# Loading and splitting all four blocks of the last gate weight inside the last expert's loop instead of one

## The chip, the cores and the metric

The kernel runs on one core of a Trainium2 chip. The metric is the device time of one execution in microseconds, the median of several executions. One further execution is profiled: its trace holds the start and the end of every instruction on every engine, every transfer, and the clock that TensorE was granted. Names of engines: PE is TensorE (PEld its weight loads), DVE is VectorE, ACT is ScalarE, POOL is GpSimd, and SP is the queue that issues the transfers.

## What is computed

The reference is a trunk of two layers for 256 tokens of width 1024 in f32. Each layer is an attention mixer, a layer norm, a channel mixer, a layer norm and a per-layer gate. Only the end of the second layer matters here: its channel mixer is a top-2-of-8 mixture of experts, and its gate is what the kernel computes last.

```
for e in range(N_EXPERTS):                                   # moe_swiglu, layer 1
    out = out + gates[..., e:e+1] * ((silu(x @ w_gate[e]) * (x @ w_up[e])) @ w_down[e])
x = layer_norm(alpha * x + out, ln_ffn_g, ln_ffn_b)
x = x + (p[i] @ w_ple_proj[i]) * sigmoid(x @ w_ple_gate[i])  # w_ple_gate[i]: 1024 x 1024
```

Each expert has three matrices of 1024 x 3584 f32, so the eight experts are the bulk of what the program reads.

## The kernel before

**Blocks and their order.** All expert weights come in blocks of 1 MB (128 partitions x 2048 f32). `main_experts` writes the order of the blocks out by hand in the list `seq`. An expert's hidden width is cut into four chunks (`CHUNKS`: 4, 8, 8 and 8 pieces of 128). A chunk of 8 pieces has eight blocks `("w", e, f, h)`, each with half a block of the gate and half of the up weight (two transfers of 512 KB, line 994), and then four blocks `("d", e, f, h)` of the down weight (one transfer each, line 121). The down blocks of a chunk stand in the list behind the w blocks of the next chunk. The step `("p", 7, 1, 0)` stands behind the down blocks of the last expert's chunk 0, and thus ahead of the w blocks of chunk 2. It carries the first of the four blocks of `w_ple_gate`, each 1 MB, which `ple_gate_blocks` lists.

**Loads.** `take(n)` issues the loads of the list, in its order, as far ahead as the ring of raw buffers has slots; `load` shrinks that ring near the end, to 18 and then to 8 slots, because the buffers are needed for other things. All loads go through one queue, SP, in program order. A load waits until the PE (or the split) has read what was in its slot.

**PE work.** Step `w` makes matmuls on L895 (`gate_up_quads`), step `d` makes matmuls on L882 and L885 (`down_quads`). `in_order` pins the order of the instructions on PE, DVE, ACT and POOL to the program's order in this loop. At the end of a chunk ACT and DVE compute silu, product and transpose (L1030 to L1035).

**Splits.** The final gate works in pairs of f32r parts: `hi` is a rounded copy made on ACT (L139), `lo` is the difference made on DVE (L143). In step `p` the first gate block is split in pieces of 1024 columns.

**The ending.** `ending` runs behind the loop. It issues the load of the second gate block, the two layer-norm parameter rows (`ln_params`, L292), and the third and fourth gate block, finishes the last down block, scatters the expert's result into `y` (L862 on PE, L865 on DVE), normalises token tile 0 (L300 to L311), transposes it (L279), and multiplies it with the gate weight (`gate_step`, L1457; token tile 1 in `gate_mm`, L1447 to L1450). Calls `high(k)` and `low(k)` put the twelve splits of the three late blocks, in pieces of 512 columns, between these operations on ACT and DVE.

Of the kernel before, what the change touches and what calls it, by code (L numbers as in the profile page):

```python
# [34 lines left out]
NE = 8  # L35
# [5 lines left out]
CB = 512  # L41
# [22 lines left out]
def trunk(ctx: ExitStack, tc: tile.TileContext, a: dict, out: bass.AP):  # L64
# [7 lines left out]
    def acc_bank(name):  # L72
        return ps.tile([P, CB], F32, tag="acc", bufs=4, name=name)

    def gu_bank(name):
        return ps.tile([P, CB], F32, tag="gu", bufs=2, name=name)
# [11 lines left out]
    rings, used = {}, {}  # L88
# [38 lines left out]
    def w_parts(loaded, piece):  # L127

        raw, nk, cols, name = loaded
        pool, tag, size = ring_slot("hl")  # L130
        hi = pool.tile([P, 2048], F32R, tag=tag + "hi", bufs=size, name=f"hi_{name}")
        lo = pool.tile([P, 2048], F32R, tag=tag + "lo", bufs=size, name=f"lo_{name}")
        n = nk * cols

        pieces = [slice(i * piece, (i + 1) * piece) for i in range(n // piece)]

        def high(i):
            cs = pieces[i]
            nc.scalar.activation(hi[:, cs], raw[:, cs], AF.Copy)  # L139

        def low(i):
            cs = pieces[i]
            nc.vector.tensor_tensor(lo[:, cs], raw[:, cs], hi[:, cs].bitcast(F32), op=ALU.subtract)  # L143

        return (hi[:, :n].rearrange("p (k c) -> p k c", c=cols),
                lo[:, :n].rearrange("p (k c) -> p k c", c=cols)), high, low

    def w_split(loaded, piece=1024):
        unit, high, low = w_parts(loaded, piece)
        for i in range(loaded[1] * loaded[2] // piece):  # L150
            high(i)
            low(i)
        return unit
# [13 lines left out]
    @contextmanager  # L167
    def in_order(engines=("PE", "DVE", "Activation", "Pool")):

        traced = nc.cur_bb.bb.instructions  # L170
        start = len(traced)
        yield
        for e in engines:
            last = None
            for ins in traced[start:]:
                if ins.engine == getattr(mybir.EngineType, e):
                    if last is not None:
                        tc.add_manual_dep(ins, last.name, mybir.DependencyInfo(
                            mybir.DependencyClass.NoSync, mybir.DependencyReason.DATA), reason="in_order")
                    last = ins  # L180
# [591 lines left out]
    def moe(i, x, xT, router, pj):  # L772
        j = i // 2
        with tc.tile_pool(name=f"route{i}", bufs=1, reuse_waits="tile") as rp:
            xT = [transposed(x[t], t, f"b{i}", rp, ("y", "zraw")[t]) for t in range(NT)]
            y = []
            hls = standing[1] + second[1]
            spare = hls[3:]
# [143 lines left out]
            def main_experts(p1, name, first):  # L922
# [2 lines left out]
                small = [r >= SMALL for r in RANKS]  # L925
                pe, peT, ob, hT = slots(0, p1, False), None, None, {}
                groups = [(CS if v else CM) // CG for v in small]
                which, loaded, hooks = {}, [], {}

                def gathered(e, h, bank):  # L930

# [20 lines left out]
                h = first(xe, pe)  # L952
# [8 lines left out]
                seq, ahead = [], None  # L961
                for e in range(NE):
                    for f, (_, nb) in enumerate(CHUNKS):
                        if ahead:

                            seq += [("w", e, f, h) for h in range(nb)]
                            seq += [("d", *ahead, h) for h in range(CHUNKS[ahead[1]][1] // 2)]
                        if (e, f) == (NE - 1, 1):
                            seq.append(("p", e, f, 0))
                        ahead = e, f  # L970
                seq += [("d", *ahead, h) for h in range(CHUNKS[ahead[1]][1] // 2)]

                def block_of(m, e, f, h):
                    if m == "p":
                        return ple_gate_blocks(i)[h]
                    if e and e not in which:
                        which[e] = nc.values_load(ordi[0:1, e:e + 1], engines=[mybir.EngineType.SP],
                                                  min_val=0, max_val=NE - 1)
                    off = which.get(e, e) * (D * DFF) + j * NE * D * DFF
                    b0, nb = CHUNKS[f]  # L980
                    if m == "d":
                        return (dram(a["w_exp_down"], off, [[1, 1]]), (b0 + 2 * h) * P, 2, D, 0, D,
                                f"d{name}{e}{f}{h}", 2 if (e, f, h) == seq[-1][1:] else 1)
                    nk = 8 // nb
                    return [dram(a[w], off + h * nk * P * DFF + b0 * P, [[DFF, P], [P * DFF, nk], [1, nb * P]])
                            for w in ("w_exp_gate", "w_exp_up")], nk, f"w{name}{e}{f}{h}"
# [10 lines left out]
                def load():  # L997

                    block, n = seq[len(loaded)], len(loaded)
                    gone = ()  # L1000
                    if n == 26:
                        gone = ("y",)
                    if n == len(seq) - 26:
                        gone = ("z", "ln", "xT0", "xT1", "w0hi", "w0lo", "w1hi", "w1lo", "w2hi", "w2lo")
                    if block[0] == "p":
                        gone = (spare[0][1] + "hi", spare[0][1] + "lo")
                    rings["raw"] = [z for z in rings["raw"] if z[1] not in gone]
                    loaded.append((gate_up_load if block[0] == "w" else w_load)(*block_of(*block)))
# [13 lines left out]
                def run(n, when):  # L1022
                    for fn in hooks.pop((n, when), []):
                        fn()
# [83 lines left out]
                with in_order():  # L1108
                    for n in range(len(seq)):
                        run(n, "pre")  # L1110
                        m, e, f, h = seq[n]
                        half = take(n)
                        run(n, "mid")
                        if n == len(seq) - 1:
                            break
                        if (m, e, f, h) == ("w", 0, 1, 3):
                            p1, gates[:] = order(gates)
                        if m == "w":
                            if h == 0:
                                banks = [acc_bank(f"w{name}{e}{f}{v}") for v in range(groups[e])]  # L1120
                            nk = half.shape[1]
                            for k in range(nk * h, nk * h + nk):
                                gate_up_quads(banks, xe, k, half[:, k % nk], k == 0, k == KD - 1)
                            if k == KD - 1:
                                token_step(e, f, banks)
                                slots_next(n, e, f)
                                if f == len(CHUNKS) - 1 and e + 1 < NE:
                                    next_expert(n, e + 1)
                        if m == "d":
                            if f == 0 and h == 0:  # L1130
                                ob = [gu_bank(f"eo{name}{e}{c}") for c in range(1 if small[e] else 2)]
                            for k in range(2 * h, 2 * h + 2):
                                edge = f == k == 0, (f, k) == (len(CHUNKS) - 1, CHUNKS[-1][1] - 1)
                                if small[e]:

                                    for r in range(2):
                                        for q in range(4):
                                            c, g = divmod(q, 2)
                                            nc.tensor.matmul(ob[0][q * CG:(q + 1) * CG, r * CQ:(r + 1) * CQ],  # L1139
                                                             hT[e, f][:, g, k, :],  # L1140
                                                             half[:, k % 2, c * CB + r * CQ:c * CB + (r + 1) * CQ],
                                                             start=edge[0] and r == 0, stop=edge[1] and r == 1)
                                else:
                                    down_quads(ob, hT[e, f], k, half, *edge)
                            if edge[1]:
                                scatter(n, e, ob, peT)
                        if m == "p":
                            rings["hl"] = [spare[0]]
                            use_slots("hl")
                            early = [w_split(loaded[n])]  # L1150
                        run(n, "post")
                    assert not hooks
                    ending(hT[seq[-1][1:3]], ob, peT, early, half)
# [267 lines left out]

            lns = []
            main_experts(pos1, "e", first_chunk)

            over = nc.values_load(left[0:1, 0:1], min_val=-C, max_val=S)
# [59 lines left out]
    loaded = [w_load(*kv[0], parts=2)]  # L1485
# [62 lines left out]
```

## Time and profile before

| | |
|---|---|
| time, median of 3 runs | 1348.99 us (1348.56 to 1349.21) |
| time of the profiled execution | 1348.58 us |
| span of the profiled execution (first to last instruction) | 1346.9 us, so 1.7 us lie around it |
| PE busy | 1311.2 us, 97% of the span |
| DVE, ACT busy | 431.6 us (32%), 318.9 us (24%) |
| SP's transfers | 434.72 MB, 82.6% of what 16 engines could carry in the span |
| mean granted clock of TensorE | 0.993 |

Times in the rows below are microseconds from the start of the span. A clock of 1.00 is 2.4 GHz, 0.50 is 1.2 GHz. The loop over the experts ends near 1299, the gate's first matmul starts at 1310.71, and the last operation on the output ends near 1337.6.

### The profile page before, as it was taken

How to read it: one execution, taken by the hardware profiler on the slowest of the kernel's cores; microseconds unless marked ns; L12 is line 12 of the kernel's file. 1: busy time of each engine (PE TensorE's matmuls, PEld its weight loads, DVE VectorE, ACT ScalarE, POOL GpSimd, SP SyncE). 2: the span in 40 equal slices, each digit the busy share in tenths (PEclk: the TensorE clock that was granted, in tenths of full speed). 3: DMA queues.
4: the chain of work that ended last, by engine and by line, in shares of the span. 5: the costliest groups of instructions: out<-in, count | busy, mean ns of one | idle time of the engine just before them, and what ended most of it. 6: DMA issues, size and time to landing. Idle time of an engine off the chain costs nothing.

```text
span 1346.9 us, 29881 instructions
## 1 busy us (share of the span) xinstructions
PE 1311.2 (97%) x12815; PEld 764.5 (57%) x12815; DVE 431.6 (32%) x843; ACT 318.9 (24%) x609; POOL 12.9 (1%) x38
## 2 busy tenths in 40 slices
PE   8999999999999999999999999999999998899986
PEld 6778888888787744453543443463543453343445
DVE  7777444445767711011010010102011011011045
ACT  6865444434458300010000000001000000001012
POOL 1000000000000000000000000000000000000000
PEclk9999999999999999999999999999999999999988
DMA  9438555535358799999999999999999999999961
GB/s 326 164 114 309 191 187 188 187 125 188 126 190 287 264 379 368 394 378 418 415 418 419 415 417 419 414 414 414 411 416 418 410 413 417 412 414 414 417 266 37
DMA packets 141364, 436.79 MB, mean 324 GB/s; under 512 B 11808, under 2 KB 12576, under 8 KB 141216
## 3 DMA queue, kind: packets, MB, share of 16 engines
q1 hardware_dynamic: 141216, 434.72, 82.6%
q8 instruction: 105, 1.72, 0.5%
q14 instruction: 43, 0.35, 0.1%
HBM read 433.63 MB, written 1.05 MB: 323 GB/s over the span
## 4 chain that ended last, share of the span: by engine, by line
PE 65%; DMA 32%; DVE 2%; issue 0%; ACT 0%; SPq 0%; DVEq 0%; ACTq 0%
DMA raw_we<-in_w_exp_up_dram 24%; PE we L895 19%; PE eoe L882 7%; DMA raw_de<-in_w_exp_down_dram 7%; PE gf L159 2%; PE gf L160 2%; PE gf L161 2%; PE uf L160 2%; PE uf L161 2%; PE uf L159 2%; PE eoe L1139 2%; PE fo L159 2%; PE fo L160 2%; PE fo L161 2%; PE qkv L161 2%; PE qkv L160 2%
## 5 line engine op out<-in xcount | busy, mean ns | idle before, releaser
L895 PE MATMUL we<-raw_we,xs_e 128*32 128x512 f32 (+1 forms) x5184 | 508.8, 545 | 7.0 <-DMA raw_we<-in_w_exp_up_dram 7.0
L895 PEld LDWEIGHTS we<-raw_we,xs_e 128*32 128x32 f32 x5184 | 166.4, 110 | 319.5 <-issue 281.8
L1033 DVE TENSOR_TENSOR sgh<-we,sgh 128x256 f32<-128x256 f32 (+1 forms) x81 | 32.0, 395 | 590.3 <-ACT sgh L1030 588.7
L882 PE MATMUL eoe<-raw_de,hT 128*32 128x256 f32 x2520 | 186.5, 379 | 0.0
L885 PE MATMUL eoe<-raw_de,hT 128*32 128x256 f32 x840 | 185.3, 379 | 0.0
L1030 ACT ACTIVATE sgh<-we 128x256 f32<-128x256 f32 (+1 forms) x81 | 29.1, 360 | 563.3 <-PE we L895 563.3
L882 PEld LDWEIGHTS eoe<-raw_de,hT 128*32 128x32 f32 x2520 | 103.6, 110 | 77.8 <-issue 5.1
L885 PEld LDWEIGHTS eoe<-raw_de,hT 128*32 128x32 f32 x840 | 92.0, 110 | 0.0
L1139 PE MATMUL eoe<-raw_de,hT 128*32 128x256 f32 x1344 | 77.0, 380 | 4.1 <-DMA raw_de<-in_w_exp_down_dram 4.1
L1139 PEld LDWEIGHTS eoe<-raw_de,hT 128*32 128x32 f32 x1344 | 42.7, 110 | 38.1 <-DMA raw_de<-in_w_exp_down_dram 5.3
L159 PE MATMUL fo<-hi_df,hTh 128*128 128x512 f32 x112 | 43.7, 390 | 0.8 <-ACT hTh L164 0.8
L143 DVE TENSOR_TENSOR lo_df<-raw_df,hi_df 128x1024 fp32r<-128x1024 f32 x28 | 33.5, 1221 | 33.8 <-ACT hi_df L139 33.8
L143 DVE TENSOR_TENSOR lo_gf<-raw_gf,hi_gf 128x1024 fp32r<-128x1024 f32 x28 | 33.2, 1221 | 34.8 <-ACT hi_gf L139 34.8
L159 PE MATMUL gf<-hi_gf,xT_b 128*128 128x512 f32 x112 | 44.2, 394 | 0.0
L161 PE MATMUL gf<-hi_gf,xT_b 128*128 128x512 f32 x112 | 43.7, 390 | 0.0
L161 PE MATMUL uf<-hi_uf,xT_b 128*128 128x512 f32 x112 | 43.7, 390 | 0.0
L159 PE MATMUL uf<-hi_uf,xT_b 128*128 128x512 f32 x112 | 43.7, 390 | 0.0
L160 PE MATMUL gf<-lo_gf,xT_b 128*128 128x512 f32 x112 | 43.6, 389 | 0.0
L160 PE MATMUL fo<-lo_df,hTh 128*128 128x512 f32 x112 | 43.6, 389 | 0.0
L160 PE MATMUL uf<-lo_uf,xT_b 128*128 128x512 f32 x112 | 43.6, 389 | 0.0
L161 PE MATMUL fo<-hi_df,hTl 128*128 128x512 f32 x112 | 43.3, 389 | 0.0
L143 DVE TENSOR_TENSOR lo_uf<-raw_uf,hi_uf 128x1024 fp32r<-128x1024 f32 x28 | 33.1, 1218 | 19.1 <-ACT hi_uf L139 19.1
(292 smaller groups left out, 1595.4 us busy)
## 6 DMA issues: line engine op xcount, KB each, us to landing
raw_de<-in_w_exp_down_dram SPq DMA_DIRECT2D x111, 1024.0 KB, 12.4
raw_we<-in_w_exp_gate_dram SPq DMA_DIRECT2D x220, 512.0 KB, 10.4
raw_we<-in_w_exp_up_dram SPq DMA_DIRECT2D x220, 512.0 KB, 10.3
raw_uf<-in_w_ffn_up_dram SPq DMA_DIRECT2D x14, 1024.0 KB, 4.9
raw_gf<-in_w_ffn_gate_dram SPq DMA_DIRECT2D x14, 1024.0 KB, 4.9
raw_df<-in_w_ffn_down_dram SPq DMA_DIRECT2D x14, 1024.0 KB, 4.8
raw_qkv<-in_w_qkv_dram SPq DMA_DIRECT2D x11, 1024.0 KB, 5.0
raw_wo<-in_w_o_dram SPq DMA_DIRECT2D x8, 1024.0 KB, 4.8
```

The source lines that it names most:

```text
L143: nc.vector.tensor_tensor(lo[:, cs], raw[:, cs], hi[:, cs].bitcast(F32), op=ALU.subtract)
L159: nc.tensor.matmul(o, xh, wh, start=start, stop=False)
L160: nc.tensor.matmul(o, xh, wl, start=False, stop=False)
L161: nc.tensor.matmul(o, xl, wh, start=False, stop=stop)
L882: nc.tensor.matmul(b[q * CG:(q + 1) * CG, c:c + CQ], xh(q), w[:, k, c0:c0 + CQ], start=start, stop=stop)
L885: nc.tensor.matmul(b[3 * CG:, c:c + CQ], xh(r), w[:, k, c0:c0 + CQ], start=start, stop=stop)
L895: nc.tensor.matmul(b[qs, :2 * nb * CG].rearrange("p (m b r) -> p m b r", m=2, b=nb), xe[:, k, g * CG:(g + 1) * CG], w[..., qs], start=firs ...
L1030: nc.scalar.activation(sg[:, g * cols:(g + 1) * cols], b[:, :cols], AF.Silu)
L1033: nc.vector.tensor_tensor(h, b[:, cols:2 * cols], h, op=ALU.mult)
L1139: nc.tensor.matmul(ob[0][q * CG:(q + 1) * CG, r * CQ:(r + 1) * CQ], hT[e, f][:, g, k, :], half[:, k % 2, c * CB + r * CQ:c * CB + (r + 1) ...
```

## The change

Steps `p` become four. Two (gate blocks 0 and 1) stand where the one stood, ahead of the w blocks of the last expert's chunk 2. Two more (blocks 2 and 3) stand behind the down blocks of chunk 1, ahead of the w blocks of chunk 3. Each step's load is issued in list order, and its split is made in the step, in four pieces of 512 columns (`CB`) where the one block was split in two of 1024. The parts of blocks 1 to 3 go into the buffers `w0` to `w2`, which leave the raw ring at the list index `len(seq) - 30` (it was `- 26`; the list is three longer). In `ending` nothing of the gate weight is left to load or to split: `late`, `pg` and `todo` are empty, and `high` and `low` do nothing.

```diff
-                which, loaded, hooks = {}, [], {}
+                which, loaded, hooks, early = {}, [], {}, []
...
-                        if (e, f) == (NE - 1, 1):
-                            seq.append(("p", e, f, 0))
+                        if e == NE - 1 and f:
+
+                            seq += [("p", e, f, h) for h in {1: (0, 1), 2: (2, 3)}.get(f, ())]
...
-                    if n == len(seq) - 26:
+                    if n == len(seq) - 30:
                         gone = ("z", "ln", "xT0", "xT1", "w0hi", "w0lo", "w1hi", "w1lo", "w2hi", "w2lo")
-                    if block[0] == "p":
+                    if block[0] == "p" and block[3] == 0:
                         gone = (spare[0][1] + "hi", spare[0][1] + "lo")
...
                         if m == "p":
-                            rings["hl"] = [spare[0]]
+                            rings["hl"] = [[spare[0], *hls[:3]][h]]
                             use_slots("hl")
-                            early = [w_split(loaded[n])]
+                            early.append(w_split(loaded[n], CB))
```

## Rows read from the trace of the kernel before

**Rows 1.** Windows: us; PE, PEld, DVE, ACT, POOL busy (instructions); clock, DMA share, GB/s.
```profile
1260.00:1265.00 5.00, 5.00 (x52) 1.54 (x48) 0.00 (x0) 0.00 (x0) 0.00 (x0) 1.00 1.03 415
...
1305.00:1310.00 5.00, 1.40 (x6) 0.78 (x5) 4.53 (x8) 0.36 (x1) 0.55 (x1) 0.50 0.00 0
```

**Rows 2.** Windows of PE alone: us, PE busy, clock, DMA share, GB/s.
```profile
1226.00:1258.00 32.00, 32.00 (x402) 1.00 1.03 414
1258.00:1294.00 36.00, 36.00 (x484) 1.00 1.02 416
```

**Rows 3.** Chain that ended last, from 1150: start, us, engine, tile, line.
```profile
1227.11 20.74 PE we L895 x192
...
1258.20 20.60 PE we L895 x192
```

**Rows 4.** Timeline of SP: start and us of single issues.
```profile
1213.37 0.89 SPq L994 DMA_DIRECT2D raw_we<-in_w_exp_up_dram  x1
...
1241.50 0.35 SPq L994 DMA_DIRECT2D raw_we<-in_w_exp_up_dram  x1
...
1264.23 0.33 SPq L994 DMA_DIRECT2D raw_we<-in_w_exp_up_dram  x1
...
1281.45 0.39 SPq L121 DMA_DIRECT2D raw_pg<-in_w_ple_gate_dram  x1
```

**Rows 5.** DMA issues, those four alone, in that order: KB, us to landing.
```profile
raw_we<-in_w_exp_up_dram SPq DMA_DIRECT2D x1, 512.0 KB, 12.8
...
raw_we<-in_w_exp_up_dram SPq DMA_DIRECT2D x1, 512.0 KB, 15.3
...
raw_we<-in_w_exp_up_dram SPq DMA_DIRECT2D x1, 512.0 KB, 9.9
...
raw_pg<-in_w_ple_gate_dram SPq DMA_DIRECT2D x1, 1024.0 KB, 16.1
```

**Rows 6.** SP's own waits, 1212 to 1280: us in total, times, longest.
```profile
SPq L121 <- PE we L895: 6.5, 4, 2.0
```

**Rows 7.** Tile raw_pg from 1299 on: ns min/median/max, first and last start.
```profile
L139 ACT ACTIVATE hi_pg<-raw_pg x12: 617/619/623, 1299.2 to 1315.7; 128x512 fp32r<-128x512 f32 x12
L143 DVE TENSOR_TENSOR lo_pg<-raw_pg,hi_pg x12: 673/684/686, 1300.0 to 1323.3; 128x512 fp32r<-128x512 f32 x12
```

**Rows 8.** Timeline of the ending and of the split in the loop: start, us, instructions.
```profile
1223.81 2.01 ACT L139 ACTIVATE hi_pg<-raw_pg 128x1024 fp32r<-128x1024 f32 x2 [1.80 <-DMA raw_we<-in_w_exp_gate_dram]
...
1299.38 0.69 DVE L165 TENSOR_TENSOR o<-eoe,o 96x512 fp32r<-96x512 f32 x1 [18.66 <-ACT o L164]
...
1299.99 1.28 DVE L143 TENSOR_TENSOR lo_pg<-raw_pg,hi_pg 128x512 fp32r<-128x512 f32 x2
...
1300.12 0.96 PE L862 MATMUL sl<-o,peT 96*128 96x512 f32 x3 [0.17 <-DVE o L165]
...
1301.19 0.74 DVE L865 SCALAR_TENSOR_TENSOR y<-sl,sm,y 128x512 f32<-128x512 f32 x1
...
1306.84 0.76 DVE L308 SCALAR_TENSOR_TENSOR z<-y,mv,ln 128x512 f32<-128x512 f32 x1
...
1308.49 1.11 PE L279 MATMUL c<-ident,z 128*128 128x128 f32 x4 [3.27 <-DVE z L311]
```

**Rows 9.** PE's waits from 1308.6 to 1336.
```profile
PE c L279 <- DVE z L311: 3.6, 2, 3.3
```

**Rows 10.** Windows of PE alone around the fall and the rise of the clock.
```profile
1301.10:1303.50 2.40, 0.00 (x0) 1.00 0.53 205
...
1310.70:1315.10 4.40, 4.40 (x13) 0.51 0.00 0
1315.10:1320.00 4.90, 4.90 (x23) 1.00 0.00 0
```

**Rows 11.** PE's waits from 1147 to 1198: us in total, times, longest.
```profile
PE we L895 <- DMA raw_we<-in_w_exp_up_dram: 4.8, 8, 0.9
```

## The prediction

> **What bounds the kernel now.** I read the windows first. In the last expert PE is busy without a gap, so the kernel looks bound by PE; but the DMA share beside it is 1.02 to 1.03 at 414 to 416 GB/s [rows 1, 2]. Both are full at once. Of two full resources, the one that can be delayed tells which has room, so I next set landings against uses. The first w block of chunk 2 is complete when its up half lands, at 1213.37 + 12.8 = 1226.2 [rows 4, 5]; PE starts on it at 1227.11 [rows 3]. The lead of the transfers is 0.9 us. For the first w block of chunk 3 it is 1241.50 + 15.3 = 1256.8 against 1258.20: 1.4 us. For the last w block of chunk 3 it is 1264.23 + 9.9 = 1274.1 against 1258.20 + 7/8 x 20.60 = 1276.2: 2.1 us. So PE never waits here, but every block comes only 1 to 2 us ahead of its use. The lead grows because a block of 1 MB takes PE 20.60 / 8 = 2.58 us and the transfers 1.0486 MB / 415 GB/s = 2.53 us. A little earlier, in an expert with less PE work, PE did wait for single blocks, by up to 0.9 us [rows 11].
>
> What is not full is the time behind the loop. The three late gate blocks are transferred there: the first is issued at 1281.45 and lands at 1297.5 [rows 4, 5], and the DMA share is 0.00 from 1305 on [rows 1]. Meanwhile a chain on DVE (scatter sums, statistics, norm) sets when the gate can start: its first transposes wait for DVE until 1308.49 [rows 8]. From there to 1336 PE waits for nothing but DVE's norm results ahead of the transposes; the splits of the gate blocks never hold it [rows 9].
>
> **The change, part by part.**
>
> *Three blocks moved ahead in the queue.* The bytes stay the same; the place changes. One more block now stands ahead of chunk 2's w blocks, and two ahead of chunk 3's. All go through SP in one order, so every later expert block lands later by 2.53 us from chunk 2 on, and by 3 x 2.53 = 7.6 us from chunk 3 on. There is no idle transfer time that would take them in [rows 2]. PE does no matmul in a p step, so it waits. At chunk 2 it waits 2.53 - 0.9 = 1.6 us. At chunk 3 the block lands at 1256.8 + 7.6 = 1264.4, and PE, itself late by 1.6, is ready at 1259.8: it waits 4.6 us. Together 6.2 us, that is 7.6 less the lead of 1.4. Behind the waiting matmul stand all of PE's remaining matmuls of the loop. The last down block would land 7.6 later, but its user is late by 6.2 with a lead of over 2, so no third wait follows. Bounds: 7.6 - 2.1 = 5.5 if the largest lead could be used, 7.6 - 0.9 = 6.7 with the smallest. I take **+6.2**, since the lead at chunk 3 is the one that stands where the blocks go in.
>
> *Slots.* The p blocks take slots in a ring of 8, and SP already waits there for PE's reads, 6.5 us in total [rows 6]. A p slot is free when its split is done, about 3 us after landing (four pieces of 0.62 on ACT, each followed by 0.68 on DVE [rows 7]); its next load stands 8 blocks later in the list, some 20 us of transfer. I cost this at nothing; if the split were so late that the queue ran dry, each block held up would cost its 2.53 us.
>
> *The ring's earlier shrink.* At index len - 30 of a list three longer, the cut falls one block earlier than before, on slots whose contents PE has long read or is about to. SP stays ahead: nothing. The loads of the norm's parameters stand behind the last down block in both versions. With the gate blocks gone from between, they land last, near 1305, as the sum of bytes is the same; they are needed at 1306.84 [rows 8] plus the shift. Hidden.
>
> *Splits in the loop.* Twelve ACT copies of 0.62 and twelve DVE differences of 0.68 [rows 7] move to a stretch in which both engines are idle (0.00 busy [rows 1]); the split there now ran from 1223.81 without holding PE [rows 8]. In-order ACT waits for each p block's landing, and behind it stand only the silus of the chunk's end, some 15 us later. Nothing; without that cover at most 3 us for each step.
>
> *Splits out of the ending.* 12 x 0.62 = 7.4 us of ACT and 12 x 0.68 = 8.2 us of DVE vanish, but only two DVE differences (1.28 us from 1299.99) lie in the chain ahead of the gate. They run between the part of `o0` (DVE until 1300.07) and the first sum into `y` at 1301.19. That sum needs PE's scatter matmuls, the second of which starts at 1300.12 and takes 0.5 [rows 8]. So the sum can start at about 1300.7, 0.5 earlier. The others lie under the gate's matmuls, which run back to back. Bounds 0 and 1.3; I take **-0.5**. The gate's matmuls on L1457 and L1447 to L1450 are unchanged in number.
>
> *TensorE's clock.* In the ending PE idles between 1301.1 and 1303.5, and from 1305 on the clock is 0.50; the gate starts at 1310.7 at half clock and gets 1.00 back at 1315.1 [rows 1, 10]. Those 4.4 us of work at 1.2 GHz cost 2.2. Single waits of up to 0.9 us left the clock at 1.00 [rows 11]. The new wait of 4.6 us is longer than either idle stretch of the ending (2.4, and 3.3 ahead of 1308.49 [rows 8, 10]), the new one of 1.6 lies between. So I expect the clock to fall once, in the long wait, and dense matmuls to follow it. Bounds: 0 (no fall), and (1315.1 - 1308.49) / 2 = 3.3, if the transposes count as well. I take **+1.5**, below the gate's 2.2 because the clock may fall late in the wait and dense work follows at once. PE cannot win it back, as it is the slower of the two afterwards. The Trainium skill, "TensorE: Matmul & The Clock Gate", section "Why this matters for your kernels", advises against idle gaps between bursts of matmuls, since an idle stretch puts the engine back to half clock; by it the time with the fall is the one to expect, and by rows 11 alone the one without.
>
> **Sum**, on the profiled execution: 1348.58 + 6.2 - 0.5 + 1.5 = **1355.8 us**. Its time is 0.4 under the median of the runs and at their lower edge, so the median of the new one may lie that much higher; I leave it at 1355.8.
>
> **The rivals.**
>
> *A: as summed*, both waits and one fall of the clock: 1354.7 to 1357.6. For it: leads of 0.9 to 2.1 against 7.6 us of added transfers. Chance 0.55.
>
> *B: the clock stays up.* The same without 1.5: 1348.58 + 5.7 = 1354.3. For it: PE was dense on both sides of the wait. Chance 0.30.
>
> *C: more than one loss of pace.* The clock falls in the wait of 1.6 as well, or slots run the queue dry for a block: 1355.8 + 1.5 to 2.5, at least 1357.3, and up to 1359. Against it: the slots are free in time by the count above. Chance 0.07.
>
> *D: largely absorbed.* The stream could take the blocks faster than 415 GB/s, or the gate's late blocks cost the ending more than its rows show, by waits that the trace puts down to other things. The net stays under 2.7 us: 1348.3 to 1351. Against it: the rate sits in the narrow band of 414 to 416 in both windows [rows 2]. Chance 0.05.
>
> *E: faster.* The loads are hidden under PE's work and the ending gets shorter: -0.5 for the chain, and -2.2 more if with less idle time the clock stays up in the ending: 1345.9. It decides if the lead were 7.6 us or more at chunk 3. The rows give 1.4. The Trainium skill, "DMA: Bandwidth & Descriptors", section "Rules for kernel authors", says to issue a transfer early, compute, and wait late; by it this change should gain. Here early issue buys nothing, because the queue in front has no gap. Chance 0.03.
>
> **How the numbers follow.** A measurement of this kernel can tell about 0.2% from no change, 2.7 us: faster is below 1346.3, slower above 1351.7. A, B and C are slower: 0.92. D holds most of "same", with part of E: 0.06; the rest of E is faster: 0.02. The range goes from B with the largest lead and twice the saving in the chain, 1348.6 + 5.5 - 1.0 = 1353.1, to A with the upper bound of the clock and some of C: 1348.6 + 6.2 - 0.5 + 3.3 = 1357.6, and 0.8 for the median and a second fall, 1358.4. It leaves out D, E and the upper part of C, under 2 in 10.
>
> **What the profile after would show.** The first matmul of chunk 2 waits about 1.6 us for the transfer of the up weight near 1227, the first of chunk 3 about 4.6 us near 1260. The last down transfer lands near 1302.6, and all transfers of the loop and the norm's rows still end near 1305. No L139 or L143 on raw_pg stands behind the loop, the first sum into `y` follows 1.3 instead of 1.8 us behind the start of `o0`'s difference, and the gate's matmuls are as dense as before. A stretch of 1.2 GHz near 1264 tells A from B. Wrong would be: no PE wait at chunk 3 (then the lead was larger than I read it), transfers ending well before 1305 (then the queue had room), or a gate phase that is shorter for want of splits.

## The result and the profile after

The kernel after the change takes **1356.65 us** (median of 4 runs, 1355.86 to 1357.74) against 1348.78 us (1348.53 to 1349.21): 7.9 us slower, a ratio of 1.0056 with a 95% interval of 1.0044 to 1.0068. The forecast was 1355.8 us, with a range of 1353.1 to 1358.4. The profiled execution is the one of 1355.86 us, with a span of 1354.1 us.

What the profile shows first is a wait. PE's waits from 1226 to 1266, the kernel after (us in total, times, longest):

```profile
PE we L895 <- DMA raw_we<-in_w_exp_up_dram: 5.9, 2, 4.6
```

The two waits are 1.3 us ahead of chunk 2 and 4.6 us ahead of chunk 3. In the kernel before, PE worked through both places without a break [rows 2, 3]. The chain that ended last, from 1220, shows the places:

```profile
1217.64 10.92 DMA raw_we<-in_w_exp_up_dram
1228.70 7.93 PE we L895 x72
...
1253.96 10.56 DMA raw_we<-in_w_exp_up_dram
1264.65 23.20 PE we L895 x192
...
1307.80 0.60 ACT o L164
```

Two things are to be read here. Chunk 3's first matmul starts at 1264.65 where it started at 1258.20 [rows 3]: 6.45 us later. And its 192 matmuls take 23.20 us where they took 20.60: 2.6 us more, with no wait inside. The windows of PE alone (us, PE busy, clock, DMA share, GB/s) say why:

```profile
1260.20:1264.60 4.40, 0.00 (x0) 0.78 1.03 419
1264.70:1269.50 4.80, 4.80 (x24) 0.50 1.01 399
1269.60:1294.00 24.40, 24.40 (x292) 1.00 1.03 417
```

The clock fell during the wait, and chunk 3's first 4.8 us ran at 1.2 GHz. The DMA share stays above 1.00 all through PE's wait: the transfers had no gap into which the gate blocks could have gone.

The ending answers to [rows 7, 8]. Tile `raw_pg` in the kernel after has all its splits in the loop (ns min/median/max, first and last start):

```profile
L139 ACT ACTIVATE hi_pg<-raw_pg x16: 612/616/630, 1223.7 to 1263.6; 128x512 fp32r<-128x512 f32 x16
L143 DVE TENSOR_TENSOR lo_pg<-raw_pg,hi_pg x16: 684/686/693, 1224.4 to 1264.5; 128x512 fp32r<-128x512 f32 x16
```

and the first sum into `y` now waits only for PE's scatter (timeline of the ending):

```profile
1308.43 0.69 DVE L165 TENSOR_TENSOR o<-eoe,o 96x512 fp32r<-96x512 f32 x1 [18.65 <-ACT o L164]
...
1309.70 0.75 DVE L865 SCALAR_TENSOR_TENSOR y<-sl,sm,y 128x512 f32<-128x512 f32 x1 [0.59 <-PE sl L862]
...
1344.17 0.43 DVE L1467 TENSOR_TENSOR z<-sig,z 128x256 f32<-128x256 f32 x1
```

It comes 1.27 us behind the start of `o0`'s difference, where it came 1.81 behind it [rows 8]: the 0.5 us of the forecast. But the whole ending, from `o0` on ACT (1307.80) to the last product on DVE (1344.17), takes 36.4 us, and in the kernel before it took 1298.75 to 1337.17, that is 38.4 us. So it won 2.0 us, not 0.5, which the experiments had to explain.

### The profile page after: what moved, and what is told of

Same layout as the page of the kernel before. It is cut to its first block, busy times and chain, and to the rows that moved or that the text cites. A ratio compares the mean times of both kernels' runs of the same rounds, so it can differ in the third digit from the quotient of the medians.

```text
span 1354.1 us, 29883 instructions
## 1 busy us (share of the span) xinstructions
PE 1313.1 (97%) x12815; PEld 767.9 (57%) x12815; DVE 432.3 (32%) x845; ACT 319.6 (24%) x611; POOL 13.4 (1%) x38
## 4 chain that ended last, share of the span: by engine, by line
PE 77%; DMA 19%; DVE 2%; ACT 1%; issue 0%; POOL 0%; SPq 0%; POOLq 0%; ACTq 0%
PE we L895 27%; DMA raw_we<-in_w_exp_up_dram 15%; PE eoe L882 9%; DMA raw_de<-in_w_exp_down_dram 4%; PE eoe L1140 3%; PE gf L159 2%; PE gf L160 2%; PE uf L159 2%; PE gf L161 2%; PE uf L160 2%; PE uf L161 2%; PE fo L159 2%; PE fo L160 2%; PE fo L161 2%; PE qkv L159 2%; PE qkv L160 2%
## 5 line engine op out<-in xcount | busy, mean ns | idle before, releaser
L895 PE MATMUL we<-raw_we,xs_e 128*32 128x512 f32 (+1 forms) x5184 | 511.4, 547 | 12.9 <-DMA raw_we<-in_w_exp_up_dram 12.7
L143 DVE TENSOR_TENSOR lo_df<-raw_df,hi_df 128x1024 fp32r<-128x1024 f32 x28 | 33.5, 1221 | 33.8 <-ACT hi_df L139 33.8
L143 DVE TENSOR_TENSOR lo_gf<-raw_gf,hi_gf 128x1024 fp32r<-128x1024 f32 x28 | 33.2, 1222 | 34.8 <-ACT hi_gf L139 34.8
L143 DVE TENSOR_TENSOR lo_uf<-raw_uf,hi_uf 128x1024 fp32r<-128x1024 f32 x28 | 33.1, 1218 | 19.1 <-ACT hi_uf L139 19.1
## 6 DMA issues: line engine op xcount, KB each, us to landing
raw_de<-in_w_exp_down_dram SPq DMA_DIRECT2D x111, 1024.0 KB, 12.5
```

Of the source, the lines that this page charges most:

```text
L895: nc.tensor.matmul(b[qs, :2 * nb * CG].rearrange("p (m b r) -> p m b r", m=2, b=nb), xe[:, k, g * CG:(g + 1) * CG], w[..., qs], start=firs ...
```

## The experiments

In the table "over before" is the difference of the medians to the kernel before in the same group of runs. "Loop end" is the start of `o0` on ACT in the run's profile, "ending" the time from there to the start of the last product on DVE, both in us.

| run | median | over before | ratio, 95% interval | loop end | ending |
|---|---|---|---|---|---|
| before, three profiles | 1348.78 to 1349.36 in four groups | | | 1298.75, 1299.36, 1299.06 | 38.4, 38.5, 38.4 |
| the change, two profiles | 1356.65 | +7.9 | 1.0056 [1.0044, 1.0068] | 1307.80, 1308.54 | 36.4, 36.5 |
| two blocks in the loop | 1351.25 | +2.0 | 1.0015 [1.0006, 1.0024] | 1301.64 | 38.6 |
| four blocks, spread | 1353.55 | +4.3 | 1.0035 [1.0023, 1.0047] | 1304.60 | 36.5 |
| the change, wait filled | 1354.20 | +4.9 | 1.0040 [1.0026, 1.0054] | 1305.66 | 37.1 |
| one more block, late in the loop | 1350.06 | +0.8 | 1.0005 [0.9996, 1.0014] | 1299.84 | 38.8 |
| no late blocks, two profiles | 1347.44 | -1.7 | 0.9985 [0.9976, 0.9994] | 1299.31, 1298.55 | 37.2, 36.2 |
| splits without transfers | 1347.40 | -1.7 | 0.9988 [0.9979, 0.9997] | 1299.03 | 37.3 |
| no differences | 1347.37 | -2.0 | 0.9984 [0.9975, 0.9993] | 1298.51 | 36.8 |
| one more block, differences later | 1348.57 | -0.8 | 0.9994 [0.9985, 1.0003] | 1300.23 | 37.3 |

**Two blocks in the loop** (from the change; blocks 2 and 3 go back to the ending):

```diff
-                            seq += [("p", e, f, h) for h in {1: (0, 1), 2: (2, 3)}.get(f, ())]
+                            seq += [("p", e, f, h) for h in {1: (0, 1)}.get(f, ())]
...
-                    if n == len(seq) - 30:
+                    if n == len(seq) - 28:
...
-                rings["hl"] = hls[:3]
+                rings["hl"] = hls[len(early) - 1:3]
```

> Only gate blocks 0 and 1 stand in the loop (both ahead of chunk 2), blocks 2 and 3 stay in the ending. Theory (each block moved ahead of a full transfer queue delays every later block by 2.53 us, PE pays that less its lead): one wait of 1.3 to 1.6 us at the first w block of chunk 2, none at chunk 3, no fall of the clock in the loop; the two DVE differences in the ending's chain stay, so nothing is won there. 1.3 to 1.6 us slower than the kernel before, near 1350.3 us. Rival (each p step costs in the loop by its own, through the in-order engines or the ring's earlier shrink, about a third of the 7.9 us that the change costs): 2.6 us slower, near 1351.4 us, without a matching wait for a transfer.

It came out 2.0 us slower, between the two, and the interval (0.8 to 3.2 us) holds both; the profile has to decide. It shows more than the one wait (PE's waits, 1220 to 1300):

```profile
PE we L895 <- DMA raw_we<-in_w_exp_up_dram: 2.3, 2, 1.2
```

The first is the expected one, 1.2 us at the first block of chunk 2. The second, 1.1 us, stands at that chunk's fourth block: its up half, issued at 1226.01, took 11.5 us to land, 1237.5, while the half ahead of it landed at 1223.57 + 11.2 = 1234.8. That is 2.7 us between two halves that otherwise land 1.25 us apart. In the kernel before, the other half of the same block was late too (1218.66 + 12.5 = 1231.2, then 1221.22 + 11.7 = 1232.9, so 1.7 us apart), but there the lead of 0.9 us covered it. So the rival's 2.6 us "without a matching wait" is out: of the loop's delay of 2.6 us (1301.64 against 1299.1, the mean of the three profiles), 2.3 lie in waits for transfers, and the rest is less than the 0.6 by which the loop end of the kernel before varies. Beside its 2.53 us, a block ahead of a full queue costs the cover against a late transfer.

**Four blocks, spread** (from the change; the four p steps stand apart):

```diff
+                            if e == NE - 1 and f > 1:
+                                seq.append(("p", e, f, {2: 1, 3: 3}[f]))
...
-                        if e == NE - 1 and f:
-
-                            seq += [("p", e, f, h) for h in {1: (0, 1), 2: (2, 3)}.get(f, ())]
+                        if e == NE - 1 and f in (1, 2):
+                            seq.append(("p", e, f, {1: 0, 2: 2}[f]))
```

> All four gate blocks stand in the loop as in the change, but apart: one behind the down blocks of chunk 0, one behind the w blocks of chunk 2, one behind the down blocks of chunk 1, one behind the w blocks of chunk 3. Theory: the same 7.6 us of transfers less the lead at the last of them (1.8 us), 5.8 us, as three waits of about 1.5, 2.1 and 2.2 us; with the chain's 0.5 us back, 5.3 us slower than before, near 1354.1 us, if waits this short leave the clock at 2.4 GHz. The kernel after the change has one wait of 4.6 us and 4.9 us of work at 1.2 GHz behind it (2.4 us lost). Rival (the fall of the clock does not come from the length of the wait): the clock falls here too and the time is near that of the change, 1356.5 us.

PE's waits from 1220 to 1300:

```profile
PE we L895 <- DMA raw_we<-in_w_exp_up_dram: 2.0, 1, 2.0
PE eoe L882 <- DVE hT L1037: 2.0, 1, 2.0
PE eoe L882 <- DMA raw_de<-in_w_exp_down_dram: 1.6, 1, 1.6
```

Three waits, 5.6 us in all, where 5.8 were expected. The second line needs care: the wait ends at 1284.45, the named transpose ends at 1284.38, and the down block that the same matmul reads, issued at 1271.64, landed 12.7 us later, at 1284.3. Both ended together, but it is the down block that held PE: in the kernel before PE goes on with the same matmuls at 1278.8, ahead of the end of that transpose at 1280.7. So all three waits are waits for transfers. The clock stays up (window of PE alone):

```profile
1220.00:1304.00 84.00, 78.36 (x1050) 1.00 0.98 398
```

The same bytes in the same loop cost 4.3 us instead of 7.9, with nearly the same sum of waits (5.6 us for 5.9). The fall of the clock in the loop belongs to the long wait, and the rival's 1356.5 us is out (the interval ends at 1355.6). The time is 1.0 us under the 5.3 that were expected, as the ending is shorter by 1.9 us and not by 0.5.

**The change, wait filled** (added to the change, behind the fourth p step):

```diff
+                            if h == 3:
+                                idle = tr_bank("idle")
+                                for m in range(16):
+                                    nc.tensor.matmul(idle, early[0][0][:, m % 4, :P], early[0][0][:, m % 4, :],
+                                                     start=m == 0, stop=m == 15)
```

> The change, with 16 matmuls of 128x512 added on PE behind the fourth p step, on parts of gate block 0, into a bank that nothing reads (some 3.7 us at 0.23 us each, inside the wait of 4.6 us ahead of chunk 3). Theory: the wait's end does not move, as the transfer sets it; the clock stays at 2.4 GHz through chunk 3, and the 2.4 us that its fall cost come back: near 1354.2 us, 5.4 us over the kernel before. Rival (the loss in chunk 3 has nothing to do with PE's idle wait): near 1356.6 us or more, as the added matmuls would come on top.

Measured: 1354.20 us, the number that was expected; over the kernel before in the same group it is 4.9 us where 5.4 was expected. The timeline of PE, and a window of PE alone behind the wait:

```profile
1260.21 3.94 PE L1155 MATMUL idle<-hi_pg 128*128 128x512 f32 x16
1264.92 1.49 PE L895 MATMUL we<-raw_we,xs_e 128*32 128x512 f32 x12 [0.77 <-DMA raw_we<-in_w_exp_up_dram]
```

```profile
1264.90:1269.90 5.00, 4.98 (x48) 1.00 1.01 404
```

The wait ends where it ended, 1264.92 against 1264.65, as the transfer sets it. But in 5.0 us PE now makes 48 matmul records where it made 24 in 4.8, and chunk 3's 192 matmuls take 20.8 us where they took 23.2. Work that nobody needs makes the kernel 2.9 us faster than the change by the medians (4.9 instead of 7.9 over before), because it keeps the engine at 2.4 GHz. The two intervals overlap, but the single executions do not: the five of the change lie 7.1 to 9.0 us over the median of the kernel before in their group, the five with the wait filled 4.6 to 5.8.

**One more block, late in the loop** (from the change):

```diff
-                            seq += [("p", e, f, h) for h in {1: (0, 1), 2: (2, 3)}.get(f, ())]
+                            seq += [("p", e, f, h) for h in {1: (0,), 3: (1,)}.get(f, ())]
...
-                    if n == len(seq) - 30:
+                    if n == len(seq) - 28:
...
-                rings["hl"] = hls[:3]
+                rings["hl"] = hls[len(early) - 1:3]
```

> Gate block 0 where the kernel before has it, block 1 behind the down blocks of chunk 2, that is ahead of the last four down blocks, and blocks 2 and 3 in the ending. One block more in the loop, as in the run with two blocks ahead of chunk 2, but at the place where the lead of the transfers is largest, 2.2 us. Theory: a wait of about 0.3 us at the first down block of chunk 3; within 0.5 us of the kernel before, near 1349.1 us. Rival (a block in the loop costs its 2.53 us, or the cost of a p step, wherever it stands): 1.4 to 2.6 us slower, near 1350.3 to 1351.4 us.

It came out 0.8 us slower, a little more than the theory's 0.5, with an interval (-0.5 to 1.9 us) that holds no change and the rival's lower end as well. The profile tells more: PE waits once in the loop, 0.4 us, at the first down block of chunk 3, as expected. The view puts this wait down to a split (L143) that ended at the same moment; the down block landed at 1289.92, and PE went on at 1290.06. Of the block's 2.53 us, 2.1 are taken by the lead. The same block ahead of chunk 2 led to two waits, 2.3 us in all. So by the waits the price of a moved transfer is its time less the lead at its place, and not a price per step.

**No late blocks** (added to the kernel before, at the start of `ending`):

```diff
+                early = early * 4
                 late = ple_gate_blocks(i)[len(early):]
```

> The kernel before without gate blocks 1 to 3: their loads and their twelve splits are left out, and the gate's matmuls use the parts of block 0 four times (so 3 MB of transfers and part of the computation are missing). Theory: the late transfers and splits lie under other work in the ending, except for two DVE differences in the chain ahead of the gate: 0.5 us faster than before, near 1348.3 us, with the gate's matmuls as dense as before. Rival (the late blocks hold the ending, and moving them away is worth something): 2 us faster or more, at most 1346.8 us.

Measured: 1.7 us faster, three times the theory's 0.5 and short of the rival's 2; the interval (0.8 to 3.2 us) leaves out the 0.5 and holds the 2. Its first profile is of the execution with the largest time of the 11, 1348.10 us, so it could not say where the gain lies.

**Splits without transfers** (from the kernel before):

```diff
-                            rings["hl"] = [spare[0]]
-                            use_slots("hl")
-                            early = [w_split(loaded[n])]
+                            early = []
+                            for m in range(4):
+                                rings["hl"] = [[spare[0], *hls[:3]][m]]
+                                use_slots("hl")
+                                early.append(w_split(loaded[n], CB))
```

> The change's splits without its transfers: only gate block 0 is loaded, in its place in the kernel before, and is split four times in the loop into the four pairs of buffers; nothing of the gate is left in the ending (3 MB of transfers are missing, the gate uses block 0 for all four). Theory: the splits in the loop lie on idle ACT and DVE and cost nothing, and the ending wins 0.5 us: near 1348.3 us, the same as the run that leaves the three blocks out altogether, with no PE wait for a transfer in the last expert. Rival (the splits in the loop hold PE, or the gate pays for them in another way): over 1349.5 us.

Measured: 1347.40 us, the same as without the blocks. Twelve splits in the loop cost nothing that shows (the loop ends at 1299.03, in the kernel before at 1298.75 to 1299.36), and PE waits for nothing in the last expert. What the change pays it pays for transfers, and for what the waits for them do to the clock. The gain is the same 1.7 us as without the blocks; the profiled execution, the slowest of the 11, has an ending that is 1.1 us shorter than before.

**The same kernels profiled again**, to see how much of the ending varies:

> The kernel before, unchanged, profiled once more: how much of the ending varies from one execution to the next. Theory (the ending's chain is fixed, only the stretch at 1.2 GHz inside it varies): from the start of o0 on ACT to the first transpose 9.7 us as in the first profile; from there to the last product on DVE 28.7 us, more or less by half of what the stretch at 1.2 GHz is longer or shorter than the 6.5 us of the first profile. Rival (the late splits hold the gate in some executions, which the first profile did not show): PE waits for L139 or L143 on raw_pg behind 1308.

> As the run before it: the kernel before, unchanged, a third profile. The same expectations: 9.7 us to the first transpose; 28.7 us from there, changed by half of the change of the stretch at 1.2 GHz; under the rival PE waits for the splits.

> The kernel without gate blocks 1 to 3 (loads and splits left out, block 0 used four times), profiled once more. Its median was 1.65 us under that of the kernel before, its one profile only 0.5. Theory (0.4 us of chain and the clock): 9.4 us from the start of o0 to the first transpose, and from there 27.8 us, changed by half of the change of the stretch at 1.2 GHz (5.3 us in the first profile). Rival (leaving the blocks out shortens the gate itself): a gate that is shorter than that rule gives by 1 us.

> The kernel after the change, unchanged, profiled once more, as its four times spread over 1.9 us. Theory: the waits of 1.3 and 4.6 us for transfers stay as they are, and the stretches at 1.2 GHz behind the long wait and in the gate differ in length from the first profile's (4.9 us of chunk 3's work, 3.5 us from the first transpose on); the time follows by half of that. Rival (the waits themselves vary): other lengths of the two waits by more than 0.3 us.

The ending of the kernel before is 38.5 and 38.4 us, as in the first profile. But "28.7 us, changed by half of the change of the stretch at 1.2 GHz" fell in both. From the first transpose to the last product the kernel before takes 28.7 us in all three profiles, although TensorE had its clock back 6.5, 5.4 and 3.9 us behind the first transpose. In the third profile that was at 1312.7 (PE alone),

```profile
1308.90:1312.60 3.70, 3.36 (x12) 0.50 0.00 0
1312.70:1320.00 7.30, 7.30 (x33) 1.00 0.00 0
```

2.3 us earlier than in the first profile [rows 10], and the ending is no shorter. The timeline of this third profile's DVE and its PE shows what took the place of the slow clock:

```profile
1315.75 2.48 DVE L143 TENSOR_TENSOR lo_pg<-raw_pg,hi_pg 128x512 fp32r<-128x512 f32 x4
1318.15 0.20 DVE L303 BATCH_NORM_AGGREGATE mv<-st 128x2 f32<-128x12 f32 x1
...
1321.09 0.75 DVE L311 SCALAR_TENSOR_TENSOR z<-z,mv,ln 128x512 f32<-128x512 f32 x1
```

```profile
1320.54 0.63 PE L279 MATMUL c<-ident,z 128*128 128x128 f32 x4 [0.30 <-DVE z L311]
1321.98 0.63 PE L279 MATMUL c<-ident,z 128*128 128x128 f32 x4 [0.82 <-DVE z L311]
```

PE stops for 0.3 and 0.8 us ahead of token 1's transposes, for token 1's norm, and the norm stands on DVE behind eight of the twelve differences. In the second profile it stops there for 0.6 us. In the first, whose clock came back last, PE and the norm arrive almost together:

```profile
1320.78 0.75 DVE L311 SCALAR_TENSOR_TENSOR z<-z,mv,ln 128x512 f32<-128x512 f32 x1
1321.02 1.29 PE L279 MATMUL c<-ident,z 128*128 128x128 f32 x8
```

PE stops there for 0.06 us only, too short to appear among the waits of [rows 9]. PE was not waiting for L139 or L143 by name, as the rival had it, but for what is queued behind L143. Without the late blocks there is no such wait, and there the theory holds: the stretch from the first transpose on follows the clock, 27.8 us where it came back after 5.3 us (first profile), 26.9 where it came back after 3.4 (second), so that the second ending takes 36.2 us. In the change it takes 27.0 and 27.1, with the clock back after 3.5 and 3.7 us.

In the change, profiled again, the waits in the loop are 1.2, 1.0 and 4.1 us, and chunk 3 again starts with about 5 us at 1.2 GHz; the extra wait of 1.0 us is of the kind that the run with two blocks showed, and the total of the waits, 6.3 us against 5.9, moved by more than the 0.3 that the theory allowed: in this point the rival was right.

**No differences** (from the kernel before; the copies and transfers stay):

```diff
-                units = early + [p[0] for p in pg]
+                units = early + [(p[0][0], p[0][0]) for p in pg]
...
-                        pg[m][2](n)
+                        pass
```

> The kernel before with only the twelve DVE differences of gate blocks 1 to 3 left out; their transfers and their ACT copies stay, and the gate uses the copy in place of the difference (part of the computation is missing). Revised theory (the ending of the kernel before is held by DVE as much as by PE: in two of its three profiles PE waited 0.6 and 1.1 us for token 1's norm, behind eight of the differences): the same gain as leaving the blocks out altogether, 1.2 to 2 us, near 1347.4 us, no PE wait for DVE at the second transposes. Rival (transfers or ACT copies held the ending): within 0.6 us of the kernel before, near 1348.7 us.

Measured: 2.0 us faster (interval 0.9 to 3.4), as much as the 1.7 of leaving the blocks out altogether. PE's waits from 1299 to 1336, in the kernel before (third profile) and here:

```profile
PE c L279 <- DVE z L311: 4.9, 4, 3.4
PE sl L862 <- ACT oh L164: 2.5, 1, 2.5
```

```profile
PE c L279 <- DVE z L311: 3.2, 2, 2.9
PE sl L862 <- ACT oh L164: 2.0, 1, 2.0
```

Two waits for the norm instead of four, and the scatter comes 0.5 us earlier. It is the twelve DVE differences, 8.2 us of an engine that is busy 21.1 of 23.8 us from 1298.75 on in the first profile, that made the ending of the kernel before longer. For the transfers and the ACT copies no loss is left that the intervals would show.

**One more block, differences later** (from the run with one more block late in the loop; a search for a kernel better than both):

```diff
-                high(2)
-                low(2)
...
                     high(1)
-                    low(1)
```

> The run with one more block ahead of the last four down blocks, and in its ending no DVE difference ahead of the first transposes: eight differences are left, four ahead of token 1's norm and four behind it. Revised theory: the wait of 0.4 us in the loop stays, the chain to the first transposes is 0.4 us shorter and token 1's norm ends some 1 us earlier: 0.5 to 1.2 us faster than the kernel before, near 1348.2 us. First theory (DVE holds the ending by 0.5 us only): 0.1 us faster at most. Rival (DVE does not hold the ending at all): as the run that it starts from, 0.8 us slower, near 1349.9 us.

Measured: 0.8 us faster than before, with an interval (0.9985 to 1.0003) that holds no change; it is inside the revised theory's range but proves nothing. The profile has the wait of 0.4 us in the loop and an ending of 37.3 us, 1.1 less than before, and PE still stops for 0.8 us for token 1's norm. No version here is clearly better than the kernel before.

## Why the prediction was right

- *"Three blocks moved ahead in the queue", +6.2:* right. The waits are 1.3 and 4.6 us where 1.6 and 4.6 were forecast, and chunk 3 starts 6.45 us late. The last down transfer lands at 1302.3 (forecast 1302.6). The waits in the spread run (5.6 us for the 5.8 expected) and in the run with a block at another place (0.4 for 0.3) bear out the rule of transfer time less lead.
- *Not foreseen:* with the lead used up, a transfer that lands late shows in PE. Waits of about 1 us of this kind appear in the two-block run and in the second profile of the change, whose 1358.03 us lie in the range of rival C ("more than one loss of pace"). What makes that one half late was not tried. A queue that ran dry is not what the trace shows: in the two-block run the DMA share is 0.99 to 1.04 in each microsecond from 1234 to 1238.
- *Slots, shrink and splits in the loop, nothing:* right; the run with the splits and without the transfers loses nothing in the loop.
- *"TensorE's clock", +1.5:* the mechanism is right, the size was too small. About 5 us of work at 1.2 GHz cost 2.6 us by the chunk's length, and 2.9 us by the medians of the change and of the run with the wait filled. So rival B, in which the clock stays up, is out. The Trainium skill, "TensorE: Matmul & The Clock Gate", section "Why this matters for your kernels", advises against idle gaps between bursts of matmuls; the trace agrees, as waits of 4.6 and 4.1 us led to the fall and in the spread run waits of up to 2.0 did not. A wait of 2.1 us elsewhere was followed by a fall too (last section).
- *"Splits out of the ending", -0.5:* too small, as the mechanism was only half seen. It measured -1.7 to -2.0. The chain ahead of the gate won 0.3 us (9.4 us from the loop's end to the first transpose where it took 9.7), close to the forecast. The step that failed is "the splits of the gate blocks never hold it", and with it "the others lie under the gate's matmuls": they rested on one profile, in which the gate's stretch at half clock ended just late enough for PE to meet DVE. In two further profiles PE waits there, for the norm behind the splits. The prediction itself had named "a gate phase that is shorter for want of splits" as a sign of being wrong, and it came: 27.0 us from the first transpose on in place of 28.7. Rival D had named such a cost of the late blocks, but with a net change under 2.7 us.

By the profiles the loop's end is later by 9.1 us (mean of two after, three before) and the ending shorter by 2.0. That leaves +7.1 at the last product, against the forecast's +7.2: two errors of opposite sign, 1.4 too little in the loop and 1.5 too little won in the ending, nearly cancel, and that the sum comes so close is luck. The medians differ by 7.9. The rest lies behind the last product, where the spans of before go on for 9.7 to 10.0 us and those of the change for 9.9 and 11.2; what made the one of 11.2 longer stays open.

## What to carry to other kernels

When two resources are both full, set landings against uses at the place where work is to be moved in: the lead there, here 1 to 2 us, is all that a transfer issued earlier can have for free. Work that is taken off a busy tail can be worth more than the chain of one profile shows, because an engine that is just behind the bound in one execution can be the bound in the next; profile the same kernel more than once. If a wait for data cannot be avoided, several short ones can cost less than a long one that lets TensorE's clock fall: here 4.3 us over before with three waits of 1.6 to 2.0 us, 7.9 with two of 1.3 and 4.6.

## What the runs showed of the hardware that was not expected

In the profile of the run with two blocks the clock fell at another place as well, in a stretch that is the same in all these kernels. Windows of PE alone:

```profile
1136.00:1144.00 8.00, 4.88 (x80) 1.00 1.02 418
1144.20:1147.50 3.30, 3.30 (x40) 0.50 1.04 413
```

A single wait of 2.1 us for a down block stands ahead of it. In the three profiles of the kernel before the longest wait there was 1.0, 1.6 and 1.7 us, and the clock stayed up. In this stretch PE follows the transfers (DMA share 1.02 to 1.04), and no delay is left of the fall 50 us later: the matmuls that wait there for a block start at 1198.55, and the same ones in the kernel before at 1198.2 to 1198.8. So a fall costs 2.6 us behind the wait in chunk 3, where PE is the slower of the two, and nothing that shows where the transfers are.
